# Strided attention on one core: keys loaded in another shape, one more store pair ahead of the reused buffers, the last two groups stored together

## The chip, the cores and the metric

The kernel runs on one core of a Trainium2 chip. Five engines work side by side: TensorE (PE), VectorE (DVE), ScalarE (ACT), GpSimd (POOL) and SyncE (SP), which here does nothing but issue transfers and wait. The transfers themselves run on the core's 16 DMA engines. The metric is the device time of one execution in microseconds. It differs from the span of the profile, which runs from the first to the last instruction of the program: in the profiled execution the time is 130.08 us and the span 128.3 us, so 1.8 us lie around the span.

## The reference

Q, K and V have shape (8, 12, 1024, 64), float32, and `stride` is 64. Every query attends to the same 16 positions:

```python
for i in range(seq):
    attend_positions = np.arange(0, seq, stride)
    q = Q[:, :, i:i + 1, :]
    k = K[:, :, attend_positions, :]
    v = V[:, :, attend_positions, :]
    scores = np.einsum('bhqd,bhkd->bhqk', q, k) * scale
    weights = np.exp(scores - np.max(scores, axis=-1, keepdims=True))
    weights = weights / (np.sum(weights, axis=-1, keepdims=True) + 1e-10)
    result[:, :, i, :] = np.einsum('bhqk,bhkd->bhqd', weights, v)[:, :, 0, :]
```

So of each of the 96 heads only 16 rows of K and of V are read, 384 KB of each in pieces of 256 bytes (one row of 64 float32). Q is read whole, 24 MB, and the output of 24 MB is written whole.

## The kernel before

The 96 heads form 24 groups of four heads, 1 MB of Q each. A group g uses the buffer `big[:, g % 16]`; its result is written into the same buffer and stored from there, so groups 16 to 23 load into buffers 0 to 7 once those are stored. Buffers 14 and 15 (`later` and `spare`) serve at the start as scratch for K and V, and take groups 14 and 15 afterwards.

Per group the work goes round the engines in this order: the cast of Q to bfloat16, half on ScalarE (`cast_a`, L341) and half on GpSimd (`cast_p`, L346); a transpose on VectorE (`turn_over`, L350); the scores on TensorE (L497); on VectorE another transpose (`spread`, L370) and the maximum (L375); the subtraction on GpSimd (L380); exp on ScalarE (L386); the sum and the reciprocal on VectorE (L391, L396); the product on GpSimd (L400); a transpose back on VectorE (`weights_back`, L406); the weighted values on TensorE (L511); and two evictions into `big` on ScalarE (L418).

The loop at L459 writes this as a software pipeline: in round n it emits, in this order, the second eviction of group n-3, `spread(n)`, `turn_over(n+1)`, `maximum(n)`, the sum of n-1, `weights_back(n-2)`, the reciprocal of n-1, `cast_p(n+2)`, the subtraction of n, the product of n-1, the placing of keys and values, `cast_a(n+3)`, exp of n, and the first eviction of n-2. Each engine works through its own instructions in that order. The class `Program` (L43) turns the named tiles each operation reads and writes into semaphore waits; a few operations count on a "gate" instead of a semaphore of their own, and where another engine has to wait for such an operation, it waits for the next one on that engine that has a semaphore, or for the gate.

Transfers are issued by SyncE alone, in the order in which they are emitted. `first_loads` (L254) issues the keys, group 0 of Q, the values, and groups 1 to 13. Groups 14 and 15 are loaded in round 0, after the value blocks, as they overwrite the scratch. Everything else follows the list `order` (L440): `("S", g)` stores groups g and g+1 as one pair of 2 MB, `("L", g)` loads group g, `("S1", 22)` stores group 22 alone. `issue` (L443) takes the next entries off this list at the end of each round, as soon as the groups that they need have been evicted. A load waits for the landing of the store of its buffer, and while SyncE waits, everything behind it in the list waits too. Group 23 is stored last, by itself, after the last eviction (L553); the kernel's final wait for the older stores does not hold this one up.

The keys: `k_raw` holds 96 rows (a head each) of 16 pieces of 64 numbers. ScalarE and GpSimd cast half of it each (L293, L296), VectorE transposes it as 32-bit words in blocks of 32 x 32 (L298), and `keys(c, s, e)` (L301) copies parts of the result to their places in `k_all`: three row blocks c by four parts s, twelve copies of 256 elements on 32 partitions, two of them on ScalarE. `keys(0, ...)` and `keys(1, ...)` come ahead of the first `turn_over`; `keys(2, ...)` comes later (L438). `place_k(g)` copies a group's keys to `k_cur`, and waits for the row block of its group, `g // 8`. The values are loaded as 128 rows of 12 pieces (L261), summed and spread by TensorE, evicted to `v_rep` and `v_rep2`, and multiplied into `v_all` by eight operations (`value_blocks`, L328).

Of the kernel before, what the change touches and what calls it, by code (L numbers as in the profile page):

```python
# [11 lines left out]
BF16 = mybir.dt.bfloat16  # L12
I16 = mybir.dt.int16
I32 = mybir.dt.int32
# [4 lines left out]
def _ap_with(ap: bass.AP, new_ap, extra_offset: int = 0) -> bass.AP:  # L19
    return dataclasses.replace(  # L20
        ap, ap=[list(p) for p in new_ap], offset=ap.offset + extra_offset
    )


def _copy(nc, out: bass.AP, in_: bass.AP):

    sides = [
        mybir.BassSymbolicTensorAccessPattern(
            ap=side.ap, dtype=side.dtype, bass_ap=side,
            is_dma=True, for_custom_bir_dma=True,  # L30
        )
        for side in (in_, out)
    ]
    return nc.sync.add_instruction(  # L34
        mybir.InstDMACopy(
            name=nc.get_next_instruction_name(), engine=mybir.EngineType.SP,
            ins=sides[:1], outs=sides[1:], queue="qSPDynamicHW",
            mode="Copy",
        )
    )  # L40


class Program:  # L43
# [123 lines left out]
def kernel(  # L167
# [8 lines left out]
    nc = tc.nc  # L176

    B, H, S, D = Q.shape
    NK = S // stride
    scale = 1.0 / math.sqrt(D)  # L180

    P = 128
    HG = 4
    NG = B * H // HG
    NH = B * H
    NC = NG // 2
    SD = S * D
    NB = 16
# [21 lines left out]
    k_all = sb.tile([P, NG, 2, 2, 32], BF16, name="k_all")  # L210
    v_all = sb.tile([P, NG, 4, D], BF16, name="v_all")
    k_cur = [sb.tile([P, 2, 2, 32], BF16, name=f"k_cur{i}") for i in range(2)]
# [3 lines left out]
    perm_v = sb.tile([P, 2, 2, 2, 2, NK], BF16, name="perm_v")  # L216

    spare, later = big[:, NB - 1], big[:, NB - 2]
    k_raw = spare[0:NH, 0 : NK * D]
    v_raw = spare[:, NK * D : NK * D + NC * D].rearrange("p (n d) -> p n d", d=D)  # L220
    later_bf = later.bitcast(BF16)
    k_bf = later_bf[0:NH, 0 : NK * D]
    k_r = later_bf[0:NH, NK * D : 2 * NK * D]
    v_bf = later_bf[:, 2 * NK * D : 2 * NK * D + NC * D].rearrange("p (n d) -> p n d", d=D)
    v_rep = later_bf[:, 3 * NK * D : 3 * NK * D + NC * D]
    v_rep2 = spare.bitcast(BF16)[:, 4 * NK * D - NC * D :]

    sc_ps = [ps.tile([P, 512], FP32, name=f"sc{i}") for i in range(2)]
    o_ps = [ps.tile([P, 2, 512], FP32, name=f"o{i}") for i in range(2)]

    prog = Program(nc, tc)
    op = prog.op

    def load(g):
        n, b = 32, g % NB
        over = {NB - 1: ["k_raw", "v_raw", "v_rep1"], NB - 2: ["k_bf0", "k_bf1", "k_r", "v_bf", "v_rep0"]}
        op("SP", lambda: _copy(
            nc, big[:, b], _ap_with(Q, [[HG * SD // n, n], [1, HG * SD // n]], g * HG * SD),
        ), writes=[f"b{b}a", f"b{b}b"] + (over.get(g) or []), lane=f"q{b}")

    def store(g, n):
        b = g % NB
        op("SP", lambda: send(g, n), lane=f"out{b // 2}",
           reads=[f"b{i % NB}{h}" for i in range(g, g + n) for h in "ab"])

    def send(g, n):
        o = big[:, g % NB : g % NB + n]
        return _copy(
            nc,
            _ap_with(out, [[16 * D, P], [2 * SD, 2 * n], [1, 16 * D]], g * HG * SD),  # L250
            _ap_with(o, [o.ap[0], [1, 1], [1, 32 * n * D]]),
        )

    def first_loads():  # L254
        op("SP", lambda: _copy(
            nc, _ap_with(k_raw, [k_raw.ap[0], [D, NK], [1, D]]),
            _ap_with(K, [[SD, NH], [stride * D, NK], [1, D]]),
        ), writes=["k_raw"], lane="out6")
        load(0)
        op("SP", lambda: nc.sync.dma_start(  # L260
            v_raw, _ap_with(V, [[stride * D, P], [2 * HG * SD, NC], [1, D]])  # L261
        ), writes=["v_raw"], lane="out7")
        for g in range(1, NB - 2):
            load(g)
# [22 lines left out]
        ), reads=["identity"], writes=["s_sel"])  # L287

    def key_rows():
        for m, (e, fn) in enumerate((("ACT", nc.scalar.copy), ("POOL", nc.gpsimd.tensor_copy))):  # L290
            part = slice(512 * m, 512 * m + 512)
            if e == "ACT":
                op(e, lambda part=part: nc.scalar.copy(k_bf[:, part], k_raw[:, part]),  # L293
                   reads=["k_raw"], writes=[f"k_bf{m}"])
            else:
                op(e, lambda part=part: nc.gpsimd.tensor_copy(out=k_bf[:, part], in_=k_raw[:, part]),  # L296
                   reads=["k_raw"], writes=[f"k_bf{m}"])
        op("DVE", lambda: nc.vector.transpose(k_r.bitcast(I32), k_bf.bitcast(I32)),  # L298
           reads=["k_bf0", "k_bf1"], writes=["k_r"])

    def keys(c, s, e):  # L301
        fn = nc.vector.tensor_copy if e == "DVE" else nc.scalar.copy
        src = k_r[32 * c : 32 * c + 32].rearrange("p (k n s f) -> p s n f k", n=8, s=4, f=2)[:, s]
        op(e, lambda: fn(k_all[32 * s : 32 * s + 32, 8 * c : 8 * c + 8, :, s % 2, NK * (s // 2) : NK * (s // 2) + NK], src),  # L304
           reads=["k_r", "k_zero"], writes=[f"k{c}{s}"])

    def value_sums(n):
        for c in range(2):
# [7 lines left out]
    def value_rows():  # L316
        op("POOL", lambda: nc.gpsimd.tensor_copy(out=v_bf, in_=v_raw), reads=["v_raw"],
           writes=["v_bf"], gate="stV")
        for n in range(2):
            op("PE", None, reads=["v_bf"] + [f"perm{n}{b}" for b in range(2)],  # L320
               writes=[f"o{n}"], gates=[("stV", 1)])
        for n in range(2):
            to = (v_rep, v_rep2)[n]
            op("ACT", lambda n=n, to=to: nc.scalar.copy(  # L324
                to.rearrange("p (c m) -> p c m", c=2), o_ps[n][:, :, 0 : NC * D // 2],
            ), reads=[f"o{n}"], writes=[f"v_rep{n}"], gate="ev")

    def value_blocks():  # L328
        for n in range(2):
            rep = (v_rep, v_rep2)[n].rearrange("p (n d) -> p n d", d=D)  # L330
            for x in range(4):
                op("DVE", lambda n=n, x=x, rep=rep: nc.vector.tensor_scalar(  # L332
                    out=v_all[:, n::2, x], in0=rep, scalar1=s_sel[:, x : x + 1], scalar2=None,
                    op0=ALU.mult,
                ), reads=[f"v_rep{n}", "s_sel"], writes=[f"v_all{n}{x}"])
# [17 lines left out]
    def place_k(g):  # L353
        op("POOL", lambda: nc.gpsimd.tensor_copy(  # L354
            out=k_cur[g % 2].rearrange("p f b x -> p (f b x)").bitcast(I32),
            in_=k_all[:, g].rearrange("p f b x -> p (f b x)").bitcast(I32),
        ), reads=["k_zero"] + [f"k{g // 8}{s}" for s in range(4)], writes=[f"k_cur{g % 2}"], gate="stK")

    def place_v(g):
        op("POOL", lambda: nc.gpsimd.tensor_copy(  # L360
# [63 lines left out]
    for s in range(4):  # L424
        keys(0, s, "DVE" if s < 2 else "ACT")
# [3 lines left out]
    for s in range(4):  # L429
        keys(1, s, "DVE")  # L430
# [4 lines left out]
    cast_a(1)  # L435
    cast_p(1)
    cast_a(2)
    for s in range(4):  # L438
        keys(2, s, "DVE")
    order = [("S", 0), ("S", 2), ("L", 16), ("L", 17), ("S", 4), ("L", 18), ("L", 19), ("S", 6),  # L440
             ("L", 20), ("L", 21), ("S", 8), ("L", 22), ("L", 23)] + [("S", g) for g in range(10, 22, 2)] + [("S1", 22)]

    def issue(done, flush=False):  # L443
        while order:
            kind, g = order[0]
            need = g + (kind == "S") if kind != "L" else g - NB + 1
            if not flush and need > done:
                return
            order.pop(0)
            if kind == "L":  # L450
                load(g)
            else:
                store(g, 2 if kind == "S" else 1)

    def on(f, g, *a):
        if 0 <= g < NG:
# [93 lines left out]
            nc.gpsimd.wait_ge(sem, n)  # L550
        nc.clear_and_free_semaphores(sems)
    tc.no_sync_barrier()
    end = send(NG - 1, 1)  # L553
    tc.declare_no_dep(end.ins, landed, reason="waits for the older stores alone")
# [1 line left out]
_INS = ['Q', 'K', 'V', 'stride']  # L556
# [31 lines left out]
```

## Time and profile before

| | us |
|---|---|
| time, median of 3 runs | 129.43 |
| lowest and highest run | 128.88, 130.23 |
| the profiled execution: time | 130.08 |
| the profiled execution: span | 128.3 |
| busy: TensorE, VectorE, ScalarE, GpSimd | 63.5, 102.3, 87.4, 87.0 |
| moved by the transfers | 51.18 MB, 399 GB/s over the span |

All times below are microseconds from the start of the span. A row of the timeline gives start, duration, engine, line of the kernel, operation, tiles written and read, and in brackets the idle time of the engine before it and what ended that. An issue row (`SPq`) gives the time that SyncE spent on issuing; the row under it, from the view of transfers, ends in the time from issue to landing. A row of the table of stages gives the stretch, the busy time of each engine, the clock granted to TensorE, the busy share of the 16 DMA engines and the rate in GB/s. A packet counts whole in the stretch in which it begins, so a share can lie a little over 1.

### The profile page before, as it was taken

How to read it: one execution, taken by the hardware profiler on the slowest of the kernel's cores; microseconds unless marked ns; L12 is line 12 of the kernel's file. 1: busy time of each engine (PE TensorE's matmuls, PEld its weight loads, DVE VectorE, ACT ScalarE, POOL GpSimd, SP SyncE). 2: the span in 40 equal slices, each digit the busy share in tenths (PEclk: the TensorE clock that was granted, in tenths of full speed). 3: DMA queues.
4: the chain of work that ended last, by engine and by line, in shares of the span. 5: the costliest groups of instructions: out<-in, count | busy, mean ns of one | idle time of the engine just before them, and what ended most of it. 6: DMA issues, size and time to landing. Idle time of an engine off the chain costs nothing.

```text
span 128.3 us, 1800 instructions
## 1 busy us (share of the span) xinstructions
PE 63.5 (49%) x580; PEld 33.6 (26%) x580; DVE 102.3 (80%) x167; ACT 87.4 (68%) x102; POOL 87.0 (68%) x132
## 2 busy tenths in 40 slices
PE   0002430338445379877777553677897777720000
PEld 0000100004222234444333222433344445510000
DVE  4666499999999999999999999999999997400000
ACT  3242756047999988888998999799888668860000
POOL 4116364299999999999999999999999867400000
PEclk9999999999999655555555999555555555685555
DMA  2989999999999899999999998999999999999991
GB/s 49 368 282 454 460 388 460 419 409 480 388 439 480 368 398 439 434 444 301 404 465 409 424 478 363 434 470 393 409 444 416 434 414 424 434 414 429 388 388 61
DMA packets 6134, 51.18 MB, mean 399 GB/s; under 512 B 3696, under 2 KB 3696, under 8 KB 3696
## 3 DMA queue, kind: packets, MB, share of 16 engines
q1 hardware_dynamic: 6128, 51.12, 95.9%
q14 instruction: 5, 0.04, 0.1%
q8 instruction: 1, 0.02, 0.0%
HBM read 25.95 MB, written 25.17 MB: 398 GB/s over the span
## 4 chain that ended last, share of the span: by engine, by line
DVE 51%; ACT 17%; PE 9%; DMA 6%; issue 6%; SPq 1%; DVEq 0%
DVE qt L350 16%; ACT big L418 13%; DVE total L391 8%; DVE w_t L406 8%; DVE s_t L370 7%; DVE top L375 7%; PE o L511 7%; DMA big<-in_Q_dram 6%; DVE v_all L332 3%; DVE rec L396 3%; ACT qb L341 2%; PE sc L497 1%; ACT big L324 1%; PE o L309 1%; SPq L34 1%
## 5 line engine op out<-in xcount | busy, mean ns | idle before, releaser
L418 ACT COPY big<-o 128x1024 f32<-128x1024 f32 x48 | 46.2, 1017 | 7.5 <-PE o L511 7.1
L511 PE MATMUL o<-v_cur,w_t 64*64 64x256 bf16 x384 | 40.0, 372 | 22.1 <-ACT big L418 12.7
L511 PEld LDWEIGHTS o<-v_cur,w_t 64*64 64x64 bf16 x384 | 29.9, 146 | 40.9 <-ACT big L418 27.8
L497 PE MATMUL sc<-qt,k_cur 128*32 128x512 bf16 x192 | 22.8, 566 | 27.7 <-DVE qt L350 27.7
L350 DVE STREAM_TRANSPOSE qt<-qb 128x1024 int32<-128x1024 int32 x24 | 28.9, 1204 | 4.1 <-ACT qb L341 2.1
L400 POOL TENSOR_TENSOR w_n<-ex,rec 128x512 bf16<-128x512 f32 x24 | 25.4, 1057 | 7.6 <-DVE rec L396 7.6
L380 POOL TENSOR_TENSOR diff<-s_t,top 128x512 f32<-128x512 f32 x24 | 25.5, 1063 | 5.8 <-DVE top L375 5.8
L346 POOL CAST qb<-big 128x1024 bf16<-128x1024 f32 x24 | 25.1, 1048 | 4.5 <-DMA big<-in_Q_dram 4.5
L341 ACT CAST qb<-big 128x1024 bf16<-128x1024 f32 x24 | 25.2, 1055 | 4.1 <-DMA big<-in_Q_dram 4.1
L386 ACT ACTIVATE ex<-diff 128x512 f32<-128x512 f32 x24 | 15.3, 637 | 7.8 <-POOL diff L380 7.8
L406 DVE STREAM_TRANSPOSE w_t<-w_n 128x512 bf16<-128x512 bf16 x24 | 18.0, 748 | 1.2 <-POOL w_n L400 1.2
L391 DVE TENSOR_REDUCE total<-ex 128x32 f32<-128x544 f32 x24 | 17.0, 710 | 0.7 <-ACT ex L386 0.7
L370 DVE STREAM_TRANSPOSE s_t<-sc 128x512 f32<-128x512 f32 x24 | 15.9, 663 | 0.0
L375 DVE TENSOR_REDUCE top<-s_t 128x32 f32<-128x512 f32 x24 | 15.6, 650 | 0.0
L497 PEld LDWEIGHTS sc<-qt,k_cur 128*32 128x32 bf16 x192 | 3.2, 104 | 37.4 <-DVE qt L350 37.4
L396 DVE RECIPROCAL rec<-total 128x32 f32<-128x32 f32 x24 | 7.5, 312 | 0.0
L354 POOL COPY k_cur<-k_all 128x64 int32<-128x64 int32 x24 | 5.9, 245 | 2.1 <-ACT k_all L304 2.1
L360 POOL COPY v_cur<-v_all 128x128 int32<-128x128 int32 x24 | 7.1, 294 | 0.0
L332 DVE TENSOR_SCALAR v_all<-big,s_sel 128x768 bf16<-128x768 bf16 x8 | 4.3, 607 | 0.0
L304 DVE COPY k_all<-big 32x256 bf16<-32x256 bf16 x10 | 3.8, 376 | 0.2
L324 ACT CAST big<-o 128x768 bf16<-128x768 f32 x2 | 1.5, 802 | 3.2 <-PE o L309 3.2
L280 DVE MEMSET k_all<- 128x1536 uint32 x1 | 1.3, 1338 | 1.9 <-issue 1.9
(17 smaller groups left out, 10.1 us busy)
## 6 DMA issues: line engine op xcount, KB each, us to landing
big<-in_Q_dram SPq DMA_DIRECT2D x24, 1024.0 KB, 14.1
out_dram<-big SPq DMA_DIRECT2D x11, 2048.0 KB, 16.1
out_dram<-big SPq DMA_DIRECT2D x2, 1024.0 KB, 11.5
big<-in_K_dram SPq DMA_DIRECT2D x1, 384.0 KB, 3.9
big<-in_V_dram SPq DMA_DIRECT2D x1, 384.0 KB, 8.6
```

The source lines that it names most:

```text
L341: op("ACT", lambda: nc.scalar.copy(b[:, half:], q[:, half:]), reads=[f"b{g % NB}{h}" for h in "ab"], writes=[f"qb{g % 4}1"])
L346: op("POOL", lambda: nc.gpsimd.tensor_copy(out=b[:, 0:half], in_=q[:, 0:half]), reads=[f"b{g % NB}{h}" for h in "ab"], writes=[f"qb{g % 4}0"])
L350: op("DVE", lambda: nc.vector.transpose(qt[g % 2].bitcast(I32), qb[g % 4].bitcast(I32)), reads=[f"qb{g % 4}0", f"qb{g % 4}1"], writes=[f"q ...
L370: op("DVE", lambda: nc.vector.transpose(s_t[g % 2].rearrange("p n k -> p (n k)"), sc_ps[g % 2],), reads=[f"sc{g % 2}"], writes=[f"s_t{g % ...
L375: op("DVE", lambda: nc.vector.tensor_reduce(out=top[g % 2], in_=s_t[g % 2], op=ALU.max, axis=mybir.AxisListType.X,), reads=[f"s_t{g % 2}"] ...
L380: op("POOL", lambda: nc.gpsimd.tensor_tensor(out=diff[g % 2], in0=s_t[g % 2], in1=top[g % 2].unsqueeze(2).to_broadcast([P, 32, NK]), op=AL ...
L391: op("DVE", lambda: nc.vector.tensor_reduce(out=total[g % 2], in_=ex[g % 2], op=ALU.add, axis=mybir.AxisListType.X,), reads=[f"ex{g % 2}"] ...
L400: op("POOL", lambda: nc.gpsimd.tensor_tensor(out=w_n[g % 2], in0=ex[g % 2][:, :, 0:NK], in1=rec[g % 2].unsqueeze(2).to_broadcast([P, 32, N ...
L406: op("DVE", lambda: nc.vector.transpose(_ap_with(w_t[g % 2], [w_t[g % 2].ap[0], [64, 8], [1, 2], [2, 32]]), w_n[g % 2].rearrange("p n k -> ...
L418: op("ACT", lambda: nc.scalar.copy(to, o), reads=[f"o{h}"], writes=[f"b{g % NB}{'ab'[h]}"], gate=None if g == NG - 1 else "ev")
L497: r = pe.matmul(sc_ps[g % 2][32 * c : 32 * c + 32], lhsT=k_cur[g % 2][:, f, b], rhs=_ap_with(qt[g % 2], [qt[g % 2].ap[0], [D, 8], [16 * D, ...
L511: r = pe.matmul(o_ps[h][half_b, t // 2, 256 * (t % 2) : 256 * (t % 2) + 256], lhsT=w_t[g % 2][half_b, 4 * h + t], rhs=v_cur[g % 2][half_b] ...
```

## The change

There are three parts. The keys are loaded as 128 rows of 12 pieces, in the shape of the values: row p holds, for each of 12 pairs of groups, one of the 16 positions of one of eight heads. The casts, the transpose and the copies follow that shape: 384 instead of 512 elements per partition, and eight copies of 384 elements in place of twelve of 256. The copies now interleave the groups: `keys(0, ...)` serves the even groups and `keys(1, ...)` the odd ones, `place_k(g)` waits for block `g % 2`, and the last four copies are gone. The scratch tiles are laid out anew, and `v_rep2` moves from buffer 15 to buffer 14.

In the list `order` three store pairs, not two, stand ahead of the load of group 16, the first into a reused buffer; the pairs behind move up by one against the loads in the same way. And the last two groups are stored as one pair at the end, where group 22 was stored alone before and group 23 at the end.

```diff
-    k_raw = spare[0:NH, 0 : NK * D]
-    v_raw = spare[:, NK * D : NK * D + NC * D].rearrange("p (n d) -> p n d", d=D)
+    k_raw = spare[:, 0 : NC * D].rearrange("p (n d) -> p n d", d=D)
+    v_raw = spare[:, NC * D : 2 * NC * D].rearrange("p (n d) -> p n d", d=D)
     later_bf = later.bitcast(BF16)
-    k_bf = later_bf[0:NH, 0 : NK * D]
...
-    v_rep2 = spare.bitcast(BF16)[:, 4 * NK * D - NC * D :]
+    k_bf, k_r, v_bf, v_rep, v_rep2 = [
+        later_bf[:, i * NC * D : (i + 1) * NC * D].rearrange("p (n d) -> p n d", d=D) for i in range(5)
+    ]
...
-        over = {NB - 1: ["k_raw", "v_raw", "v_rep1"], NB - 2: ["k_bf0", "k_bf1", "k_r", "v_bf", "v_rep0"]}
+        over = {NB - 1: ["k_raw", "v_raw"], NB - 2: ["k_bf0", "k_bf1", "k_r", "v_bf", "v_rep0", "v_rep1"]}
...
-            nc, _ap_with(k_raw, [k_raw.ap[0], [D, NK], [1, D]]),
-            _ap_with(K, [[SD, NH], [stride * D, NK], [1, D]]),
+            nc, k_raw, _ap_with(K, [[stride * D, P], [2 * HG * SD, NC], [1, D]]),
...
+        op("ACT", lambda: nc.scalar.copy(k_bf[:, 0:6], k_raw[:, 0:6]), reads=["k_raw"], writes=["k_bf0"])
+        op("POOL", lambda: nc.gpsimd.tensor_copy(out=k_bf[:, 6:], in_=k_raw[:, 6:]),
+           reads=["k_raw"], writes=["k_bf1"])
...
     def keys(c, s, e):
         fn = nc.vector.tensor_copy if e == "DVE" else nc.scalar.copy
-        src = k_r[32 * c : 32 * c + 32].rearrange("p (k n s f) -> p s n f k", n=8, s=4, f=2)[:, s]
-        op(e, lambda: fn(k_all[32 * s : 32 * s + 32, 8 * c : 8 * c + 8, :, s % 2, NK * (s // 2) : NK * (s // 2) + NK], src),
-           reads=["k_r", "k_zero"], writes=[f"k{c}{s}"])
+        src, b, u = 32 * (2 * c + s // 2), s % 2, s // 2
+        op(e, lambda: fn(
+            k_all[32 * s : 32 * s + 32, c::2, :, b, NK * u : NK * u + NK],
+            k_r[src : src + 32].rearrange("p n (a k f) -> p a n f k", a=2, f=2)[:, b],
+        ), reads=["k_r", "k_zero"], writes=[f"k{c}{s}"])
...
-        ), reads=["k_zero"] + [f"k{g // 8}{s}" for s in range(4)], writes=[f"k_cur{g % 2}"], gate="stK")
+        ), reads=["k_zero"] + [f"k{g % 2}{s}" for s in range(4)], writes=[f"k_cur{g % 2}"], gate="stK")
...
-    for s in range(4):
-        keys(2, s, "DVE")
-    order = [("S", 0), ("S", 2), ("L", 16), ("L", 17), ("S", 4), ("L", 18), ("L", 19), ("S", 6),
-             ("L", 20), ("L", 21), ("S", 8), ("L", 22), ("L", 23)] + [("S", g) for g in range(10, 22, 2)] + [("S1", 22)]
+    order = [("S", 0), ("S", 2), ("S", 4), ("L", 16), ("L", 17), ("S", 6), ("L", 18), ("L", 19), ("S", 8),
+             ("L", 20), ("L", 21), ("S", 10), ("L", 22), ("L", 23)] + [("S", g) for g in range(12, 22, 2)]
...
-                store(g, 2 if kind == "S" else 1)
+                store(g, 2)
...
-    end = send(NG - 1, 1)
+    end = send(NG - 2, 2)
```

More of the change, by code (lines that the diff above doesn't have):

```diff
@@ L218 @@
     spare, later = big[:, NB - 1], big[:, NB - 2]
-    k_raw = spare[0:NH, 0 : NK * D]
-    v_raw = spare[:, NK * D : NK * D + NC * D].rearrange("p (n d) -> p n d", d=D)
+    k_raw = spare[:, 0 : NC * D].rearrange("p (n d) -> p n d", d=D)
+    v_raw = spare[:, NC * D : 2 * NC * D].rearrange("p (n d) -> p n d", d=D)
     later_bf = later.bitcast(BF16)
-    k_bf = later_bf[0:NH, 0 : NK * D]
-    k_r = later_bf[0:NH, NK * D : 2 * NK * D]
-    v_bf = later_bf[:, 2 * NK * D : 2 * NK * D + NC * D].rearrange("p (n d) -> p n d", d=D)
-    v_rep = later_bf[:, 3 * NK * D : 3 * NK * D + NC * D]
-    v_rep2 = spare.bitcast(BF16)[:, 4 * NK * D - NC * D :]
+    k_bf, k_r, v_bf, v_rep, v_rep2 = [
+        later_bf[:, i * NC * D : (i + 1) * NC * D].rearrange("p (n d) -> p n d", d=D) for i in range(5)
+    ]
     sc_ps = [ps.tile([P, 512], FP32, name=f"sc{i}") for i in range(2)]
@@ L289, in key_rows @@
     def key_rows():
[L290 to L299, printed above, removed]
+        op("ACT", lambda: nc.scalar.copy(k_bf[:, 0:6], k_raw[:, 0:6]), reads=["k_raw"], writes=["k_bf0"])
+        op("POOL", lambda: nc.gpsimd.tensor_copy(out=k_bf[:, 6:], in_=k_raw[:, 6:]),
+           reads=["k_raw"], writes=["k_bf1"])
+        op("DVE", lambda: nc.vector.transpose(
+            k_r.rearrange("p n d -> p (n d)").bitcast(I32), k_bf.rearrange("p n d -> p (n d)").bitcast(I32),
+        ), reads=["k_bf0", "k_bf1"], writes=["k_r"])
     def keys(c, s, e):
         fn = nc.vector.tensor_copy if e == "DVE" else nc.scalar.copy
-        src = k_r[32 * c : 32 * c + 32].rearrange("p (k n s f) -> p s n f k", n=8, s=4, f=2)[:, s]
-        op(e, lambda: fn(k_all[32 * s : 32 * s + 32, 8 * c : 8 * c + 8, :, s % 2, NK * (s // 2) : NK * (s // 2) + NK], src),
-           reads=["k_r", "k_zero"], writes=[f"k{c}{s}"])
+        src, b, u = 32 * (2 * c + s // 2), s % 2, s // 2
[3 more added lines that the diff above has]
+        ), reads=["k_r", "k_zero"], writes=[f"k{c}{s}"])
     def value_sums(n):
@@ L324, in value_rows @@
             op("ACT", lambda n=n, to=to: nc.scalar.copy(
-                to.rearrange("p (c m) -> p c m", c=2), o_ps[n][:, :, 0 : NC * D // 2],
+                to.rearrange("p (c n) d -> p c (n d)", c=2), o_ps[n][:, :, 0 : NC * D // 2],
             ), reads=[f"o{n}"], writes=[f"v_rep{n}"], gate="ev")
@@ L329, in value_blocks @@
         for n in range(2):
-            rep = (v_rep, v_rep2)[n].rearrange("p (n d) -> p n d", d=D)
+            rep = (v_rep, v_rep2)[n]
             for x in range(4):
```

## The prediction

> **What bounds the kernel now.** I read the page's head, slices and queues first:
>
> ```profile
> span 128.3 us, 1800 instructions
> DMA  2989999999999899999999998999999999999991
> q1 hardware_dynamic: 6128, 51.12, 95.9%
> DVE 51%; ACT 17%; PE 9%; DMA 6%; issue 6%; SPq 1%; DVEq 0%
> ```
>
> The last row is the chain of waits, and it names VectorE. But the chain follows instructions and ends at ScalarE's last eviction (114.5, below); the span ends 14 us later. The queue's row says why: the 16 transfer engines are busy 95.9% of the span, nearly flat from the second slice to the last but one. The bound is the queue, so a gain must come from its idle share, or from its start or its end. I looked for that next, in the table of stages (last two columns: share of the 16 engines, GB/s):
>
> ```profile
> 11.70:44.00 32.30, 13.65 (x132) 5.38 (x132) 30.12 (x50) 21.25 (x25) 23.23 (x32) 0.98 1.01 435
> 58.00:62.00 4.00, 3.14 (x32) 1.56 (x24) 4.00 (x8) 3.65 (x5) 3.71 (x6) 0.50 0.92 307
> 62.00:114.00 52.00, 35.66 (x332) 20.36 (x328) 47.76 (x78) 45.55 (x54) 43.24 (x63) 0.63 1.00 427
> 119.00:124.60 5.60, 0.00 (x0) 0.00 (x0) 0.00 (x0) 0.00 (x0) 0.00 (x0) 0.50 0.99 417
> 124.60:125.60 1.00, 0.00 (x0) 0.00 (x0) 0.00 (x0) 0.00 (x0) 0.00 (x0) 0.50 0.43 180
> 125.60:126.60 1.00, 0.00 (x0) 0.00 (x0) 0.00 (x0) 0.00 (x0) 0.00 (x0) 0.50 0.20 82
> ```
>
> Loads alone run at 435 GB/s, so 1 MB (1.049 million bytes) takes 2.4 us. Two places lose time. At 58 to 62 the rate is 307 against 427 around it: 4 x (1 - 307/427) = 1.1 us. And at the end the share falls to 0.43 and then 0.20: 0.20 of 16 is three engines, which work on for about 2.5 us after the other 13 are done at 124.6. Every transfer is dealt to all engines alike, so these three fell behind earlier. Where? The start (issue rows; time from issue to landing as the last figure; the chain's row for the first Q load; and the casts that waited for the second and third):
>
> ```profile
> 0.96 0.76 SPq L34 DMA_DIRECT2D big<-in_K_dram  x1
> big<-in_K_dram SPq DMA_DIRECT2D x1, 384.0 KB, 3.9
> 1.78 7.70 DMA big<-in_Q_dram
> 13.77 1.04 POOL L346 CAST qb<-big 128x1024 bf16<-128x1024 f32 x1 [1.61 <-DMA big<-in_Q_dram]
> 16.17 1.04 POOL L346 CAST qb<-big 128x1024 bf16<-128x1024 f32 x1 [1.36 <-DMA big<-in_Q_dram]
> ```
>
> K lands at 0.96 + 3.9 = 4.9. Q0 should follow 2.4 us later, at 7.3; it lands at 1.78 + 7.70 = 9.5. That is 2.2 us lost, about what the three engines are behind at the end. Q1 is there by 13.7: 4.2 us after Q0, and V lies between, so V (384 KB in 256-byte pieces) costs 4.2 - 2.4 = 1.8 us. Q2 follows 2.4 us behind Q1: nothing lost there. With stores at 4.9 us a pair (rows below) the queue's work after Q0 is 1.8 + 23 x 2.4 + 12 x 4.9 = 115.8, so from 9.5 to 125.3; the last landing is at 127.5, and 1.1 of the 2.2 us between lie at 58 to 62.
>
> **The change, part by part.** The store rows:
>
> ```profile
> 105.00 0.54 SPq L34 DMA_DIRECT2D out_dram<-big  x1
> out_dram<-big SPq DMA_DIRECT2D x1, 2048.0 KB, 12.7
> 113.59 0.54 SPq L34 DMA_DIRECT2D out_dram<-big  x1
> out_dram<-big SPq DMA_DIRECT2D x1, 2048.0 KB, 9.0
> 114.17 0.60 SPq L34 DMA_DIRECT2D out_dram<-big  x1
> out_dram<-big SPq DMA_DIRECT2D x1, 1024.0 KB, 10.9
> 115.50 0.64 SPq L34 DMA_DIRECT2D out_dram<-big  x1
> out_dram<-big SPq DMA_DIRECT2D x1, 1024.0 KB, 12.0
> 110.72 3.76 ACT big L418 x4
> ```
>
> *The last two groups as one pair.* Store 18 lands at 117.7 and store 20 at 122.6: 4.9 us a pair. The two single stores land at 125.1 and 127.5, 2.4 to 2.5 each: two of them cost what a pair costs. SyncE saves one issue of 0.6 us; the pair is issued after the last eviction (114.5) where the single one of group 23 was, near 115.5, and has until 122.6, when store 20 is through: cover 7 us. So 0. The Trainium skill (DMA: Bandwidth & Descriptors, "Anatomy of one DMA") gives each transfer a fixed cost of about 2.0 us on the path it describes, by which one transfer less would end the kernel 2.0 us earlier; the 2.4 us between the two landings, half a pair, says that this cost lies beside the other transfer and is not to be had.
>
> *K as 128 rows of 12 pieces.* 96 x 16 and 128 x 12 are both 1,536 pieces of 256 bytes. The new form is that of the V load line for line, priced above at 1.8 us. If K takes 1.8 us as well, the start is as before: 0. But what makes Q0 late right behind K the trace does not show. So this term has two ends: -2.2 if the old form is the cause, and +2.2 if the new form sets engines back by as much again. I take 0: V, the nearest row, neither gains nor loses against its neighbours. The Trainium skill (DMA: Bandwidth & Descriptors, "Latency and other measured facts") reports copies with a 2 MiB row pitch at 164 instead of 207 GB/s; K's 12 pieces of a row now lie 2 MB apart, so by it K would take 1.8 x 207/164 = 2.3 us and the sum would be +0.5. V has that pitch now, and its 1.8 us contain whatever that costs.
>
> *Casts, transpose and copies of the keys.* The rows of the start on VectorE:
>
> ```profile
> 5.62 0.71 DVE L298 STREAM_TRANSPOSE big<-big 96x512 int32<-96x512 int32 x1 [1.11 <-POOL big L296]
> 6.36 2.28 DVE L304 COPY k_all<-big 32x256 bf16<-32x256 bf16 x6
> 10.66 1.25 DVE L350 STREAM_TRANSPOSE qt<-qb 128x1024 int32<-128x1024 int32 x1 [2.02 <-POOL qb L346]
> 11.93 1.61 DVE L304 COPY k_all<-big 32x256 bf16<-32x256 bf16 x4
> 16.34 1.25 DVE L350 STREAM_TRANSPOSE qt<-qb 128x1024 int32<-128x1024 int32 x1 [2.06 <-ACT qb L341]
> ```
>
> Per partition the casts and the transpose shrink from 512 to 384 elements (0.71 becomes 0.53 to 0.71), and the six early copies grow from 256 to 384 elements: 2.28 us becomes 2.28 to 3.42. They end between 8.4 and 9.8 instead of 8.6, ahead of the first Q transpose at 10.66, which waits for Q0's cast: hidden, 0. The four later copies (1.61 us) go, but the next Q transpose at 16.34 waits 2.06 us for ScalarE's cast, so VectorE only waits longer: 0. Were Q0 2.2 us earlier, the copies would be late by up to 1.3 us, still inside what the queue hides. The value tile v_rep2 moves, so load 14 waits for the second half of the value blocks as well:
>
> ```profile
> 21.08 0.47 SPq L34 DMA_DIRECT2D big<-in_Q_dram  x1
> big<-in_Q_dram SPq DMA_DIRECT2D x1, 1024.0 KB, 24.3
> ```
>
> It goes out some 1.3 us later, and stood 24.3 us in the queue: 0.
>
> *Three store pairs ahead of load 16.* The bytes in the queue are the same, but each of loads 16 to 23 now has one more pair ahead of it and lands 4.9 us later. SyncE issues store 4 before it waits for store 0's landing, store 6 before loads 18 and 19, and so on; and the loads stand some 12 us in the queue already (rows below), so nothing runs dry. Who needs them? Loads 20 and 22 are the tightest (landing = start + last figure):
>
> ```profile
> 68.75 0.47 SPq L34 DMA_DIRECT2D big<-in_Q_dram  x1
> big<-in_Q_dram SPq DMA_DIRECT2D x1, 1024.0 KB, 12.2
> 78.56 0.47 SPq L34 DMA_DIRECT2D big<-in_Q_dram  x1
> big<-in_Q_dram SPq DMA_DIRECT2D x1, 1024.0 KB, 12.1
> 84.91 1.06 ACT L341 CAST qb<-big 128x1024 bf16<-128x1024 f32 x1
> 92.43 1.06 ACT L341 CAST qb<-big 128x1024 bf16<-128x1024 f32 x1
> 93.38 0.64 ACT L386 ACTIVATE ex<-diff 128x512 f32<-128x512 f32 x1
> 95.57 0.71 DVE L391 TENSOR_REDUCE total<-ex 128x32 f32<-128x544 f32 x1
> ```
>
> Load 20: 80.9 + 4.9 = 85.8, cast at 84.91: 0.9 late. Load 22: 90.7 + 4.9 = 95.6, cast at 92.43: 3.2 late. Behind that cast ScalarE's queue holds exp of group 19; VectorE's sum of group 19 needs it. Exp ends at 94.0 and the sum begins at 95.57, so 1.6 us are in hand: the 0.9 (the same steps two groups earlier) are covered, of the 3.2 VectorE waits 1.6 us. VectorE sets the pace of what follows (the chain of waits), so all of it moves by 1.6 us. Store 20 waits for the third of the last four evictions, and goes out at 115.2 instead of 113.59. Is that on the path? The 13 engines that are ahead began store 20 about 4.9 + 4.9 us before 124.6, at 114.8: they now idle for 1.6 us. The three that set the end reach it 2.5 us later, at 117.3, when it has long been issued. So the end does not move: 0, and what is late next is the 13 engines, about 126.2 instead of 124.6, still under 127.1. The cover left is 0.9 us.
>
> **Sum:** 0 on the profiled 130.08 us, so no change on the median of the three runs, 129.43, which lies 0.65 below it. I predict 129.4.
>
> **Rivals.** *The start's loss goes with the old key load.* For: the 2.2 us vanish just behind the only transfer of 96 rows; V, of the new form, lets Q1 follow without loss. Against: K is also the first transfer of the program, and the dip at 58 to 62 has no key load near it. All engines would then end together: 129.4 - 2.2 = 127.2; the loads would land 2.2 us earlier too, so VectorE's wait disappears.
>
> *Slower, by the loads.* The cover of 0.9 us is thin. If loads 20 to 22 slip by 2.5 us beyond the 4.9 (two more dips like that at 58 to 62), cast, exp and store 20 slip with them, and the end moves by 2.5 - 0.9 = 1.6: 131.0. It decides from a store 20 issued after 116.1. Against it: from 62 to 114 the rate holds at 427.
>
> *Slower, by the key load:* the new form puts engines back by another 2.2 us, 131.6. For: strided pieces over all of K. Against: V's price.
>
> **Chances.** Forecast 0.47 (own range 128.3 to 130.5, the 2.2 us lost after Q0 shrinking or growing by half), the start's loss gone 0.31, slower by the loads 0.10, slower by the key load 0.12. A difference under 1%, 1.3 us, cannot be told from none. Faster takes the first rival and a little of the forecast's edge, 0.32; slower both others, 0.21; within 1%, 0.47. The range reaches from just under the first rival to the loads' rival: 126.9 to 131.1.
>
> **What would show it.** K landing 3.9 us after its issue and Q0 at 9.5 again, with three engines working alone for 2.5 us at the end: forecast. Q0 at about 7.3 and a last share that falls at once: first rival. Loads 20 and 22 landing near 85.8 and 95.6, ScalarE's cast waiting for Q there, VectorE's sum waiting for exp once, by 1.6 us, store 20 out at 115.2: the order's step is right. A queue share under 0.9 between 62 and 114 would prove me wrong on the order, and a pair at the end that takes other than 4.9 us on the last step.

## The result and the profile after

The changed kernel takes 128.53 us (median of 20 executions, 128.34 to 129.09); the kernel before takes 130.0 us in 20 executions, from 128.88 to 132.10. The ratio is 0.9896, with a 95% interval of 0.9875 to 0.9917: 1.0% faster. Here and below, ratios leave out executions more than 1.5% above the fastest of their kernel, while ranges and medians take in all, as the scatter is itself what the experiments look into. The two ranges say more than the medians: one of the 20 executions before (128.88) lies inside the range of the changed kernel, and the other 19 lie above it, by up to 3 us.

The head, slices, queue and chain of the changed kernel:

```profile
span 126.7 us, 1795 instructions
DMA  0999899899998989999899999989989999999991
q1 hardware_dynamic: 5984, 51.12, 96.3%
DVE 28%; ACT 26%; DMA 19%; PE 10%; issue 7%; SPq 0%; DVEq 0%
```

The queue is still the bound, 96.3% busy in a span that is 1.6 us shorter. The profiled execution takes 128.58 us. The stages (last two columns: share of the 16 transfer engines, GB/s):

```profile
11.70:44.00 32.30, 14.65 (x136) 6.10 (x130) 28.92 (x47) 21.55 (x26) 23.05 (x32) 1.00 1.01 433
58.00:62.00 4.00, 2.90 (x24) 1.56 (x24) 4.00 (x8) 3.64 (x6) 3.71 (x6) 0.50 1.07 446
62.00:112.00 50.00, 34.85 (x320) 19.94 (x320) 47.22 (x77) 43.38 (x52) 42.65 (x62) 0.61 1.00 425
118.00:124.00 6.00, 0.00 (x0) 0.00 (x0) 0.00 (x0) 0.00 (x0) 0.00 (x0) 0.50 0.99 423
124.00:125.00 1.00, 0.00 (x0) 0.00 (x0) 0.00 (x0) 0.00 (x0) 0.00 (x0) 0.50 0.16 66
```

Two things differ. The dip at 58 to 62 is gone: 446 GB/s instead of 307. And the tail is shorter: after 124 the share is 0.16, two or three engines. A landing is counted in 16 steps, one for each transfer engine, and the trace has the time of each step: the last store lands from 124.5 to 125.9 here, from 125.0 to 127.5 before. The start, with issue rows, landings, and the casts that wait for Q1 and Q2:

```profile
0.95 0.73 SPq L34 DMA_DIRECT2D big<-in_K_dram  x1
big<-in_K_dram SPq DMA_DIRECT2D x1, 384.0 KB, 4.8
1.74 0.83 SPq L34 DMA_DIRECT2D big<-in_Q_dram  x1
big<-in_Q_dram SPq DMA_DIRECT2D x1, 1024.0 KB, 6.5
12.05 1.04 POOL L341 CAST qb<-big 128x1024 bf16<-128x1024 f32 x1 [0.93 <-DMA big<-in_Q_dram]
14.48 1.04 POOL L341 CAST qb<-big 128x1024 bf16<-128x1024 f32 x1 [1.39 <-DMA big<-in_Q_dram]
```

K lands later than before, 5.8 instead of 4.9, and yet Q0 lands earlier, at 8.2 instead of 9.5: it follows K by 2.4 us, the time of its own bytes. The 2.2 us that were lost between the two are gone, of which 0.9 went into K itself. That leaves 1.3 us at the start; at the last landing the difference is 1.6 us, 125.9 instead of 127.5.

The rows that answer to those on the loads, the last stores and the casts:

```profile
74.77 0.92 SPq L34 DMA_DIRECT2D big<-in_Q_dram  x1
big<-in_Q_dram SPq DMA_DIRECT2D x1, 1024.0 KB, 18.6
93.42 1.04 ACT L336 CAST qb<-big 128x1024 bf16<-128x1024 f32 x1 [1.45 <-DMA big<-in_Q_dram]
113.05 0.54 SPq L34 DMA_DIRECT2D out_dram<-big  x1
out_dram<-big SPq DMA_DIRECT2D x1, 2048.0 KB, 8.0
114.31 0.54 SPq L34 DMA_DIRECT2D out_dram<-big  x1
out_dram<-big SPq DMA_DIRECT2D x1, 2048.0 KB, 11.6
```

Load 22 lands at 93.4, 2.7 us later than before, and ScalarE's cast waits 1.45 us for it. VectorE's sums do not wait there, and store 20 goes out at 113.05. The last pair lands 4.9 us behind store 20.

### The profile page after: what moved, and what is told of

Its sections match the earlier page's. It is cut to its first block, busy times and chain, and to the rows that moved or that the text cites. A ratio compares the mean times of both kernels' runs of the same rounds, so it can differ in the third digit from the quotient of the medians.

```text
span 126.7 us, 1795 instructions
## 1 busy us (share of the span) xinstructions
PE 63.7 (50%) x580; PEld 33.6 (27%) x580; DVE 101.4 (80%) x163; ACT 86.9 (69%) x102; POOL 86.9 (69%) x132
## 3 DMA queue, kind: packets, MB, share of 16 engines
q1 hardware_dynamic: 5984, 51.12, 96.3%
## 4 chain that ended last, share of the span: by engine, by line
DVE 28%; ACT 26%; DMA 19%; PE 10%; issue 7%; SPq 0%; DVEq 0%
ACT big L413 20%; DMA big<-in_Q_dram 15%; PE o L504 8%; DVE qt L345 8%; DMA big<-in_K_dram 4%; DVE total L386 4%; DVE s_t L365 3%; DVE top L370 3%; DVE w_t L401 3%; ACT qb L336 3%; DVE v_all L327 3%; DVE k_all L297 2%; ACT ex L381 2%; PE sc L490 1%; ACT big L319 1%
## 5 line engine op out<-in xcount | busy, mean ns | idle before, releaser
L297 DVE COPY k_all<-big 32x384 bf16<-32x384 bf16 x6 | 2.9, 489 | 0.1
```

## The experiments

All ratios are to the kernel before in executions on the same chip. The expectations speak of theory A (the key load), B (the order) and so on; each letter is explained where it first stands.

### The three parts one by one

**The key part alone**: the changed kernel with the old order and the old last stores.

```diff
     order = [("S", 0), ("S", 2), ("L", 16), ("L", 17), ("S", 4), ...] + [("S1", 22)]
...
     end = send(NG - 1, 1)
```

> The key part alone (load as 128 rows, eight copies, new scratch layout); order of the stores and the two single stores as before. Theory A (the gain comes from the start: with the old key load three transfer engines fall behind and stay behind): ratio to before near 0.990, Q0 lands at about 8.2, Q0 to the last store no engine more than 1.5 us behind. Theory B (the gain comes from the order of stores and loads, the dip at 58 to 62 being a cost of the switch from stores to loads): ratio 1.00 and the dip at 58 to 62 is still there.

Measured: 128.56 us (128.48 to 128.83, 6 executions) against 131.09 (129.43 to 132.25), ratio 0.981 (0.977 to 0.985).

```profile
1.75 0.83 SPq L34 DMA_DIRECT2D big<-in_Q_dram  x1
big<-in_Q_dram SPq DMA_DIRECT2D x1, 1024.0 KB, 6.0
58.00:62.00 4.00, 2.90 (x24) 1.56 (x24) 4.00 (x8) 3.64 (x5) 3.72 (x6) 0.50 0.92 389
```

Q0 lands at 7.8, the stretch from 58 to 62 runs at 389 GB/s although the order is the old one, and the whole gain is there. So the gain comes with the key load, as theory A has it, and the ratio is better than expected because the kernel before is slower on this chip. But the way from the start to the end is not that of theory A. It expected no engine more than 1.5 us behind at the last store; there the first engine lands at 124.0 and the last at 126.2, although they were only 0.5 us apart at Q0. The spread has grown again on the way, to nearly that of the kernel before (125.0 to 127.5). What has moved most is the first engine: level at Q0 (7.2 before, 7.3 here), it is 1.0 us ahead at the end, and it won that in the stretch of the dip, where load 17 took it 2.4 us instead of 3.2. Reckoned by the first engine, 1.0 of the 1.3 us between the last landings of these two profiles thus comes from the dip.

**The order alone**, on the kernel before.

```diff
-    order = [("S", 0), ("S", 2), ("L", 16), ("L", 17), ("S", 4), ("L", 18), ...
+    order = [("S", 0), ("S", 2), ("S", 4), ("L", 16), ("L", 17), ("S", 6), ("L", 18), ...
```

> Before with the new order alone (three store pairs ahead of load 16). Theory A: ratio 1.000, three engines still 1.5 to 4 us behind at the end; load 22 lands near 95.6, VectorE's sum waits once by about 1.6 us and store 20 goes out near 115, without moving the end. Theory B: ratio near 0.990.

Measured: 129.54 us (128.29 to 130.79, 6 executions), ratio 0.984 (0.979 to 0.990). This I had not expected. The profiled execution took 130.5 us:

```profile
76.00 0.93 SPq L34 DMA_DIRECT2D big<-in_Q_dram  x1
big<-in_Q_dram SPq DMA_DIRECT2D x1, 1024.0 KB, 19.4
95.41 1.05 ACT L341 CAST qb<-big 128x1024 bf16<-128x1024 f32 x1 [2.63 <-DMA big<-in_Q_dram]
97.02 0.72 DVE L391 TENSOR_REDUCE total<-ex 128x32 f32<-128x544 f32 x1 [0.70 <-ACT ex L386]
115.04 0.54 SPq L34 DMA_DIRECT2D out_dram<-big  x1
58.00:62.00 4.00, 3.14 (x31) 1.62 (x32) 4.00 (x8) 3.63 (x5) 3.71 (x6) 0.50 1.03 438
```

What the prediction worked out for the order is all there: load 22 at 95.4, the cast waiting, VectorE's sum waiting for exp, store 20 at 115.04. It was 0.70 us of waiting in VectorE and not 1.6. But the dip at 58 to 62 has gone too (438 GB/s), and that the prediction did not have. It does not show up as time in this profile, whose last store lands at 127.9.

**The last pair alone**, on the kernel before.

```diff
-    end = send(NG - 1, 1)
+    end = send(NG - 2, 2)
```

> Before with the last two groups stored as one pair. Theories A and B: ratio 1.000 (between 0.998 and 1.002); the last pair lands 4.9 us behind store 20. A fixed cost of about 2 us for each transfer that is not hidden would give 0.985.

Measured: 130.62 us (128.93 to 132.10, 12 executions), ratio 0.996 (0.991 to 1.001). The profiled execution took 131.2 us; it shows the old key load in the old order a second time:

```profile
58.00:62.00 4.00, 1.94 (x32) 0.94 (x24) 4.00 (x8) 3.75 (x5) 3.72 (x6) 0.97 0.91 291
114.14 0.54 SPq L34 DMA_DIRECT2D out_dram<-big  x1
out_dram<-big SPq DMA_DIRECT2D x1, 2048.0 KB, 9.6
115.41 0.54 SPq L34 DMA_DIRECT2D out_dram<-big  x1
out_dram<-big SPq DMA_DIRECT2D x1, 2048.0 KB, 13.2
```

The pair lands at 128.6, 4.9 us behind store 20 at 123.7, and the dip at 58 to 62 is there again. The pair is worth nothing that can be measured.

**The new keys and the pair in the old order.**

> The changed kernel with the old order (two store pairs ahead of load 16). Theory A: ratio to before 0.990, as the changed kernel; with the engines together at the start the loads land early enough in both orders, and the order is worth nothing (within 0.3%). Theory B: ratio 1.00. If the new order costs VectorE a wait that moves store 20, this kernel is faster than the changed one by up to 0.6 us (0.985).

Measured: 128.79 us (128.47 to 128.91, 6 executions), ratio 0.982 (0.978 to 0.986). With the new keys the order is worth at most 0.3 us; no cost of the new order is seen. So the order and the keys seem to remove partly the same loss: with either of them changed as here, the stretch from 58 to 62 runs at 389 GB/s or more.

### What it is about the key load

**V first.** On the kernel before, the order of issue is V, Q0, K, Q1.

> Before with the issue order of the start turned round: V (128 rows), Q0, K (96 rows), Q1. Theory A1 (the form with 96 rows sets engines back): Q0 lands evenly (last engine under 1 us behind the first) about 2.4 us behind V, and Q1, behind K, is spread by 2 us or more. Theory A2 (whatever is transferred first sets engines back): Q0, behind V, is spread by 2 us or more, and Q1 follows K without further loss. Computing begins some 2 us later in both, so the time says less than the landings.

Measured: ratio 1.015 (1.009 to 1.022). V lands at 4.9 and Q0 at 8.1, with 1.3 us between the first and the last of the 16 engines; Q1 is even. Neither transition loses 2 us, so in this one profile neither theory is borne out. Two things in it limit what follows. Q1 lands within 0.4 us on all engines although K, in its old form, is right ahead of it: the old form does not set back every load behind it. And the dip at 58 to 62 is there although the engines are together (0.6 us apart at the landing of store 0, at 50.9):

```profile
58.00:62.00 4.00, 3.07 (x28) 1.59 (x24) 4.00 (x8) 3.63 (x6) 3.71 (x6) 0.50 0.92 320
```

The time tells little, as store 20 goes out at 116.9 because computing begins late.

**Rows and distance.** The old load differs from the new in two main ways: 96 rows or 128, and pieces of a row 16 KB or 2 MB apart. (The rows themselves lie 256 KB apart in the old load and 16 KB in the new; the runs at 1 MB and 1.5 MB have the rows 16 KB apart as well.) The runs cross these, each with one changed access pattern:

```diff
-            _ap_with(K, [[SD, NH], [stride * D, NK], [1, D]]),                   # before
+            _ap_with(K, [[stride * D, NH], [NH * stride * D, NK], [1, D]]),      # 96 rows, 1.5 MB
+            _ap_with(K, [[stride * D, NH], [HG * SD, NK], [1, D]]),              # 96 rows, 1 MB
+            _ap_with(K, [[stride * D, NH], [2 * HG * SD, NC], [1, D]]),          # 96 rows of 12, 2 MB
+            _ap_with(K, [[SD, NH], [stride * D, NC], [1, D]]),                   # 96 rows of 12, 16 KB
-            nc, k_raw, _ap_with(K, [[stride * D, P], [2 * HG * SD, NC], [1, D]]),   # after
+            nc, k_raw, _ap_with(K, [[NC * stride * D, P], [stride * D, NC], [1, D]]),   # 128 rows, 16 KB
+            nc, k_raw, _ap_with(K, [[stride * D, P], [NH * stride * D, NC], [1, D]]),   # 128 rows, 1.5 MB
```

> Before, with K read as 96 rows of 16 pieces that lie 1.5 MB apart in place of 16 KB (the pieces land in the wrong rows, so the keys are mixed; the work is the same). Theory A1 (row count): ratio to before 1.00, K lands after 3.9 us or more, Q0 spread by 2 us or more as before. Theory A3 (distance of the pieces in memory): ratio near 0.985, K lands after about 4.8 us and Q0 is spread by under 1 us, as with the changed kernel.

> The changed kernel, with K read as 128 rows of 12 pieces that lie 16 KB apart in place of 2 MB (the keys are mixed; the work is the same). Theory A1 (row count): ratio to before near 0.985, Q0 spread by under 1 us. If the distance makes K's landing late (4.8 instead of 3.9 us), K lands after about 3.9 us here. Theory A3 (distance): ratio 1.00 and Q0 spread by 2 us or more.

> The changed kernel, with the 12 pieces of a row of K 1.5 MB apart in place of 2 MB (some rows are read twice, others not at all, so the keys are mixed; the work is the same). Theory A3b (what counts is that pieces exactly 2 MB apart are read slowly, so that K lands at 4.8 us after its issue on all engines and Q0 starts evenly behind it): K lands after about 3.9 us, and the executions scatter over more than 1.5 us, as before, median over 129.3. Theory A1 (128 rows): executions within 0.9 us of each other, median 128.5.

> Before, with K read as 96 rows of 12 pieces 2 MB apart (a quarter of the pieces is not loaded but cleared, the keys are mixed; everything behind is as before). Theory A3b: K lands after 4 to 4.8 us, executions within about 1 us, ratio to before near 0.985. Theory A1: K lands after 3.5 to 3.9 us, executions scatter as before, ratio 0.995 to 1.00.

> Before, with K read as 96 rows of 16 pieces 1 MB apart (all 1,536 pieces, some rows twice, others not at all; the keys are mixed, the work is the same). In the run with 96 rows of 12 pieces 2 MB apart fewer pieces were read, so the row count was not cleanly set aside. Theory D (distance of the pieces, whatever the rows): if 1 MB acts like 2 MB, executions lie within 1 us of each other, median 128.5; if it acts like 1.5 MB, they scatter over 2 us or more, median 129.5 to 130.5, K lands 3.9 us after its issue. Theory F (fewer pieces made that run even): scatter as before.

> Before, with K read as 96 rows of 12 pieces 16 KB apart: as many pieces as in the run with 12 pieces 2 MB apart, at the old distance (the last four pieces of each row are not loaded but cleared). Theory D2 (2 MB between the pieces evens the start): executions scatter over 2 us or more as before, median 129.3 to 130.5. Theory F (fewer pieces even it): executions within 1 us of each other, median 128.5.

Measured, with the parts above for comparison (Q0's landing is from the one profile of each kernel, the range from all its executions):

| key load | kernel | executions | range, us | median | Q0 lands |
|---|---|---|---|---|---|
| 128 x 12, 2 MB | after | 20 | 128.34 to 129.09 | 128.53 | 8.2 |
| | keys alone | 6 | 128.48 to 128.83 | 128.56 | 7.8 |
| | keys and pair | 6 | 128.47 to 128.91 | 128.79 | 8.0 |
| 96 x 12, 2 MB | | 6 | 128.11 to 128.88 | 128.47 | 7.7 |
| 96 x 16, 16 KB | before | 20 | 128.88 to 132.10 | 130.00 | 9.5 |
| | pair alone | 12 | 128.93 to 132.10 | 130.62 | 9.7 |
| | order alone | 6 | 128.29 to 130.79 | 129.54 | 10.1 |
| 96 x 12, 16 KB | | 6 | 128.51 to 129.80 | 129.46 | 9.4 |
| 96 x 16, 1 MB | | 6 | 128.26 to 131.67 | 130.38 | 9.6 |
| 96 x 16, 1.5 MB | | 10 | 128.35 to 132.17 | 130.12 | 8.4 |
| 128 x 12, 16 KB | | 4 | 128.34 to 130.71 | 129.83 | 8.4 |
| 128 x 12, 1.5 MB | | 12 | 128.36 to 130.32 | 129.16 | 10.0 |

The rows come from several chips, on which the kernel before itself has medians from 129.84 to 131.09; the run of 96 x 12 at 2 MB and those at 1.5 MB and of 128 x 12 at 16 KB are from one chip. Every kernel of the table whose pieces lie 2 MB apart stays within 0.8 us and its Q0 lands by 8.2. Every other one scatters by 1.3 to 3.8 us, and its Q0 lands at 8.4 to 10.1. The row count does not divide them: 96 rows are even at 2 MB, 128 rows scatter at 16 KB and at 1.5 MB. So theory A1 falls and the distance of 2 MB is what the even kernels have in common. Reading fewer pieces takes some of the scatter away as well (96 x 12 at 16 KB: 1.3 us), but not the 1 us in the median. A kernel that scatters is not late in every execution: the two profiles with Q0 at 8.4 took 128.38 and 129.05 us, the six with Q0 at 9.4 or later 129.47 to 131.2. That suggests that the executions scatter as Q0's landing does; one profile of each kernel does not show it. The table also says more of the dip. It stands in the old order with pieces 16 KB or 1 MB apart (96 x 12 at 16 KB, then 96 x 16 at 1.5 MB, the profile with Q0 at 8.4, where it does not):

```profile
58.00:62.00 4.00, 2.35 (x32) 0.94 (x24) 4.00 (x8) 4.00 (x6) 3.71 (x6) 1.00 0.83 311
58.00:62.00 4.00, 2.90 (x24) 1.58 (x24) 4.00 (x8) 3.64 (x5) 3.70 (x6) 1.00 0.93 393
```

The issue rows of 128 x 12 at 1.5 MB, then those of 96 x 12 at 2 MB:

```profile
big<-in_K_dram SPq DMA_DIRECT2D x1, 384.0 KB, 3.9
1.74 0.83 SPq L34 DMA_DIRECT2D big<-in_Q_dram  x1
big<-in_Q_dram SPq DMA_DIRECT2D x1, 1024.0 KB, 8.3
```

```profile
big<-in_K_dram SPq DMA_DIRECT2D x1, 288.0 KB, 3.9
1.78 0.71 SPq L34 DMA_DIRECT2D big<-in_Q_dram  x1
big<-in_Q_dram SPq DMA_DIRECT2D x1, 1024.0 KB, 5.9
```

K as a whole lands later with pieces 2 MB apart, 4.4 to 4.8 us after its issue in four profiles against 3.8 to 4.1 in seven at the smaller distances, and with three quarters of the bytes 3.9 against 3.7. Q0 behind it is on time all the same.

**Is it enough that the small pieces last longer?** The kernel before, with the old key load issued twice.

```diff
+        again = big[0:NH, 13, 0 : NK * D]
+        op("SP", lambda: _copy(
+            nc, _ap_with(again, [again.ap[0], [D, NK], [1, D]]),
+            _ap_with(K, [[SD, NH], [stride * D, NK], [1, D]]),
+        ), writes=["b13a", "b13b"], lane="out5")
```

> Before, with the old load of K issued twice in a row, the second copy into the buffer of group 13, where it is overwritten later and not used. It adds 1.8 us of transfer. Theory C (what evens the start is only that the small pieces last long enough to cover the time until Q0's pieces can all start, as the slower pieces of the new load do): executions within about 1 us of each other and Q0 spread by under 1 us; the time is at most 1.8 us above the changed kernel, 128.5 to 130.3. Theory D (it is the distance of the pieces itself): executions scatter over 2 us or more and the median is 1.5 to 2 us above before.

Measured: 132.66 us (130.36 to 133.73, 6 executions) beside 129.84 for before.

```profile
2.64 1.74 SPq L34 DMA_DIRECT2D big<-in_Q_dram  x1
big<-in_Q_dram SPq DMA_DIRECT2D x1, 1024.0 KB, 8.9
```

Q0 lands at 11.5, 4.9 us behind the second K (6.7), and the executions scatter by 3.4 us. Theory C falls: a longer stretch of small pieces does not help.

**Q0 first**, on the kernel before and on the changed one.

```diff
     def first_loads():
+        load(0)
         op("SP", lambda: _copy(
...
-        load(0)
```

> Before, with group 0 of Q issued ahead of K. Theory S (the loss at the start is engines that wait for Q0's pieces while the queue is still being fed with the 1,536 pieces of K): with Q0 in front nothing waits, Q0 lands near 5 us, K near 7, V near 9, the executions lie within 1 us, ratio 0.98 to 0.99. If the loss sits with whatever large transfer meets the small pieces, Q1 is spread instead and the ratio stays at 1.00.

> The changed kernel with group 0 of Q issued ahead of K. Theory S: Q0 lands near 5 us; the transfers have about 1 us less to lose, but store 20 goes out near 113 or later as in the changed kernel, so the time is 127.5 to 128.5. If the copies of the keys now hold up the start (K near 7.5), store 20 goes out by up to 1.5 us later and the time is that of the changed kernel or up to 1 us longer.

Measured: 129.86 us (129.42 to 131.07, 12 executions), ratio 0.999 (0.995 to 1.003), and 129.66 (129.28 to 131.09, 12 executions), ratio 1.005 (1.000 to 1.009). In the kernel before:

```profile
big<-in_Q_dram SPq DMA_DIRECT2D x1, 1024.0 KB, 5.3
9.37 3.06 DVE L304 COPY k_all<-big 32x256 bf16<-32x256 bf16 x6
12.44 1.25 DVE L350 STREAM_TRANSPOSE qt<-qb 128x1024 int32<-128x1024 int32 x1
115.65 0.54 SPq L34 DMA_DIRECT2D out_dram<-big  x1
117.56 0.65 SPq L34 DMA_DIRECT2D out_dram<-big  x1
out_dram<-big SPq DMA_DIRECT2D x1, 1024.0 KB, 10.2
```

Q0 is there at 6.3, and V, now right behind K in its old form, lands within 0.5 us on all engines, so the loss behind K is gone, as theory S had it; the scatter is halved with the old key load. But now K is late, the key copies end at 12.4 and hold up the first Q transpose by 1.8 us, and store 20 goes out at 115.65. The last store lands 12.1 us after that. From 112 to 120 the engines' share is only 0.78 to 0.85: here computing, not the transfers, sets the end, and an earlier start of one transfer was paid for by a later start of the other. The changed kernel with Q0 first is alike: store 20 goes out at 114.9 instead of 113.05, and the last store lands at 127.2.

### What ends last now

The changed kernel with store 20 issued as soon as group 21 is evicted.

```diff
         on(evict, n - 3, 1)
+        if n == NG:
+            op("ACT", lambda: nc.scalar.copy(edge[:, 0:1], edge[:, 1:2]), writes=["edge"])
...
-        issue(n - 3 if n + 3 < NG else n - 4)
+        issue(n - 3 if n + 3 < NG or n == NG else n - 4)
```

> The changed kernel, with store 20 issued as soon as group 21 is evicted (a one-column copy on ScalarE behind that eviction gives SyncE something to wait for) and not behind the first eviction of group 23. Theory E (with the engines even, store 20 out at 113.05 is what ends last for most of them: it leaves them idle for some 0.6 us): store 20 goes out near 110.8, the time falls by 0.3 to 0.7 us to 127.8 to 128.2. If the one or two engines that lag by 1.3 us at the end set the time, it stays at 128.5.

Measured: 128.57 us (128.37 to 128.83, 12 executions), as the changed kernel.

```profile
109.88 0.54 SPq L34 DMA_DIRECT2D out_dram<-big  x1
out_dram<-big SPq DMA_DIRECT2D x1, 2048.0 KB, 11.0
114.38 0.54 SPq L34 DMA_DIRECT2D out_dram<-big  x1
out_dram<-big SPq DMA_DIRECT2D x1, 2048.0 KB, 11.4
124.00:125.00 1.00, 0.00 (x0) 0.00 (x0) 0.00 (x0) 0.00 (x0) 0.00 (x0) 0.50 0.16 66
```

Store 20 goes out 3.2 us earlier and lands at 120.9, as in the changed kernel (121.0), and the end stays at 125.8. Theory E falls: the two or three engines that lag at the end set the time, not the issue of store 20. They had not lagged so at the start: the 16 engines are 0.8 us apart at Q0 and 1.9 at the last store.

## Why the prediction was right or wrong

The forecast was no change and the time fell by 1.0%; the first rival had the right place and sign, at 127.2 for a measured 128.5. Its "All engines would then end together" did not come: they are 1.5 us apart at the last landing.

- **What bounds the kernel.** Right. The queue, the three engines that lag, and the 2.2 us between K and Q0 were the places where time went, and so was the dip. The end was read too simply: nine engines land the last store by 125.3, four by 126.3 and three at 127.4 to 127.5, not 13 at 124.6. And I took the profiled execution for the kernel. Before, the executions scatter from 128.4 to 132.6 over all the chips used, and the three times that I had, 128.88 to 130.23, were a hint of that which I read as noise.
- **"K as 128 rows of 12 pieces", taken at 0: wrong, and this is the step that failed.** The whole change measured -1.5 us in the medians over 20 executions, and the key part alone is as fast (128.56 us); in the profiles its span is 1.3 us shorter, that of the whole change 1.6. I set V beside it as the nearest row, and V could not tell: what matters is not what the load costs but what the load behind it loses. Q0 follows K by 2.4 us instead of 4.6. The rival that had this tied it to the 96 rows; the runs tie it to the 2 MB between the pieces. The same step left out a second gain: the dip, 1.1 us in the prediction and taken to have nothing to do with the keys, goes with the key part alone, and reckoned by the first engine it makes 1.0 of those 1.3 us.
- **The rule of the Trainium skill** (DMA: Bandwidth & Descriptors, "Latency and other measured facts", on the 2 MiB pitch) gave +0.5 us, an estimate. The rule is on the pitch between the rows of a copy; here the pieces of one row lie 2 MB apart and the rows 16 KB, so it was carried over. K does land later, by 0.5 to 0.9 us (4.4 to 4.8 after its issue, 3.9 before), but the time did not rise, as Q0 behind it lost less.
- **The rival of +2.2 by the new form** did not occur in any of the 44 executions with the new load ahead of Q0.
- **Casts, transpose and copies at 0.** Right. The six copies on VectorE took 3.02 us, between the two bounds. With Q0 early they end at 10.06 and the first Q transpose follows at 10.09, so they have just become what it waits for; nothing of that reaches the end, which in the changed kernel does not hang on when store 20 goes out (the run with store 20 early).

```profile
7.04 3.02 DVE L297 COPY k_all<-big 32x384 bf16<-32x384 bf16 x6
10.09 1.25 DVE L345 STREAM_TRANSPOSE qt<-qb 128x1024 int32<-128x1024 int32 x1
```

- **The order at 0.** Right with the new keys, where the two runs in the old order lie within 0.3 us of the changed kernel. Wrong with the old keys: alone it gave 0.984, and the dip at 58 to 62 went with it. That this is the cause is not shown, as the one profile without the dip is of an execution of 130.5 us. I had priced the dip at 1.1 us and treated it as an accident. It stands in six profiles, all in the old order with pieces 16 KB or 1 MB apart (291 to 340 GB/s); in the old order it is missing with 2 MB (389 to 418), with 1.5 MB (393) and with Q0 first (397), and in all six profiles with the new order (438 to 455). The wait that the order adds came where it was put: in the run of the order alone load 22 was predicted at 95.6 and landed at 95.4, store 20 at 115.2 and went out at 115.04. VectorE waited 0.70 us where I had 1.6, as that execution ran some 0.7 us late by then.
- **The pair at 0.** Right: 4.9 us behind store 20, alone 0.996 (0.991 to 1.001).
- **The loads as a slower rival.** Its starting point, a store 20 out after 116.1, was not reached in the profile of any kernel with the new order and the keys ahead of Q0.

Open remains why pieces 2 MB apart let Q0 through evenly. That K lands later is measured; that this is the cause is not, since a longer stretch filled with more pieces 16 KB apart does not do it. The distance is not the whole of it either: with V or Q0 ahead of K, the load behind the old K was even. Open too is what makes the dip at 58 to 62, and how the key load, over by 6, acts on it 50 us later; the lag of the engines does not explain it, as the run with V first has the dip without the lag.

## What to carry to other kernels

When the queue is the bound, look at the engines one by one: a share that falls to 3/16 at the end says that a few of them lost time earlier, and what to look for is that loss, not the last transfer. Follow the first and the last engine through the landings: a lag from the start and one picked up on the way end in the same tail. A load is priced by what lands behind it as well as by its own landing; a slower one can be the better one. And where a handful of times spread by 1%, the spread itself is a loss that a change can remove: compare ranges, not only medians.

## What the runs showed of the hardware that I had not expected

- Where K is the first load and Q0 comes right behind it, the distance in memory between K's 256-byte pieces goes with how Q0 starts. Behind pieces 2 MB apart Q0 landed at 7.7 to 8.2 in each of five profiles; behind pieces 16 KB, 1 MB or 1.5 MB apart at 8.4 to 10.1 in eight, and the executions scattered by 1.3 to 3.8 us instead of 0.4 to 0.8. With V or Q0 issued ahead of K, the load behind pieces 16 KB apart landed within 0.5 us on all 16 engines.
- A lag stays while the queue has work: before, three engines were 2.2 us behind the first at Q0 and three were 2.4 to 2.5 us behind it at the last store, 118 us later; every landing is counted by all 16. New lags arise on the way (0.5 us at Q0 and 2.2 at the end in the key part alone). When the queue runs short, the lag goes: with 128 x 12 at 1.5 MB the engines' share fell to 0.48 from 114 to 118, with store 20 out at 115.6, and the 3.3 us between the engines at load 22 were 0.5 at the landing of store 20.
- In the old order, the stretch from 58 to 62 ran at 291 to 340 GB/s in six profiles with K's pieces 16 KB or 1 MB apart and at 389 to 418 in five others; with one more store pair queued ahead it ran at 438 to 455 in all six.
